# Seven raw weight buffers in place of four, in an encoder layer on one Trainium2 core

## The chip, the core and the metric

The kernel runs on one core of a Trainium2 chip. The core has a matrix engine (TensorE; PE in the profile, PEld for its weight loads), a vector engine (VectorE, DVE), a scalar engine (ScalarE, ACT), GpSimd (POOL), a queue engine that issues most transfers (SyncE, SP), and 16 DMA engines. The metric is the device time of one execution in microseconds (us), the median of several runs.

## What is computed

One layer of a hybrid streaming encoder, in float32, on 2048 prompt tokens and 128 sample tokens (8 sequences of 16), model width 1024:

```python
qm, km, vm, om, ip, fp, qa, ka, va = split_in(x @ w_in)
hm = sigmoid(om) * head_norm(mlstm_chunkwise(qm, km, vm, ip, fp))   # 4 heads of 128, matrix memory
ha = window_attention(rope(qa), rope(ka), va, attn_sinks)           # 8 q heads, 2 kv heads of 64, window 128
mix = concatenate([hm, ha]) @ w_out
h = layer_norm(ALPHA * x + mix)
u = h @ w_up                                                        # 1024 -> 2 * 2816
a, g = split(causal_conv(u, w_conv, b_conv))                        # width 3, per channel
y = layer_norm(ALPHA * h + (silu(g) * a) @ w_down)                  # 2816 -> 1024
```

The prompt starts from empty states, the sample from given ones (mLSTM state, key and value cache, last convolution rows). Outputs are y and the new states of both.

## The kernel before

**Tiles and stages.** The 2176 tokens are 17 tiles of 128. Four stages follow one another. (i) The *input projection* (some 0 to 620 us of the profile): four blocks of four tiles, the sample's with the first; per block five groups of columns and seven products per group (`i_product`, L704). The mLSTM, the attention and the sample's own work are woven between the products. (o) The *output projection* and the first layer norm (to about 900 us). (f) The *up-projection* with convolution and gate (about 900 to 1840 us): three blocks of tiles, 22 pairs of value and gate columns in each, seven products per pair (L1873). (d) The *down-projection* and second norm (to the end): three blocks, seven products, six units of the inner dimension in each (L2083).

**Precision and products.** A float32 product is made of three matmuls on reduced-precision parts (`mm3`): each operand is split into a high part (ScalarE casts, L217) and a low part (VectorE subtracts, L218). The large projections use schemes with seven block products in place of eight, so some of their operands are sums of quarters of a weight matrix or of the tokens. Sums that later blocks need again are kept in HBM (`zws`, `zw`, `zt`); `d_sums` (L844 to L856) makes those of w_down during stage (i), from loads of w_down into tiles `txy`.

**The way of a weight.** SyncE loads 4 KB per partition of raw weights into a tile of the tag `wraw`. L217 and L218 split it into two tiles of the tags `wlo` and `whi` (named w or uw; four buffers each, two more in an extra pool), and PE reads those. The raw tile is free again when the split has ended, the split tiles when PE has used them. Four places take a `wraw` tile:
- `warm_up` (L320), once, at the start;
- `raw_slot` (L405), which stages (i) and (o) use for w_in, the gate columns, w_out, kept sums and one sum of tokens (L547);
- `f_raw` (L1769), two tiles for each pair of stage (f): value weights `wv` (loaded at L1770) and gate weights `wg` (L1772, L1774), of which L1790 to L1793 form sums in the first block;
- `d_weights` (L2016), one for each unit of stage (d), loaded at L2019 five units ahead.

In stage (i) some raw tiles are also changed in place (L505, L508, L510, L522), where sums are formed.

**What sets the order.** The order of PE's instructions is written out by hand: a class `Chains` interleaves the chains of mLSTM, attention and sample with the products by costs and due times. For stages (i) and (o) the program asks for raw tiles ahead of their use: `next_raw` walks a list of weight units, and `raw_free` allows a request only when the older of the last four raw tiles are marked as done. The orders of VectorE, ScalarE, GpSimd and SyncE aren't written out: a list scheduler lays them down at build time, with its own estimates of durations, from the dependences and from when buffers come free. Each engine and each queue then runs its instructions in that order; an instruction that waits holds up all behind it.

**Beside the weights.** SyncE's queue also carries stores and reloads of everything that passes through HBM: projected queries, keys and gates, tokens, the first norm's inputs (L1635) and its gains (L1646), convolution rows (`cc`, `zc`), gated results (`zf`, reloaded as `r`). GpSimd issues three kinds of transfers itself: `zM` (L1078), which writes a row of the mLSTM's sums to HBM, `wi` (L1080), which broadcasts it back to all partitions and is read by VectorE's L1109, each 16 times, and finished tiles of y (L2126), 12 times.

**The instructions named by the prediction.** L771, L775, L777 (evictions of a product's bank in stage (i)), L761 (gates), L871 (rotary); L1132, L1150 to L1159 (the mLSTM's scores and head norm); L1307 to L1320 (softmax of the prompt's attention); L1501 to L1511 and L1517 (softmax and transposes of the sample's); L1902 to L1910 (convolution of stage (f)); L1894 (its gate).

[...]

Of the kernel before, what the change touches and what calls it, by code (L numbers as in the profile page):

```python
# [8 lines left out]
F32 = mybir.dt.float32  # L9
# [5 lines left out]
P = 128  # L15
D = 1024
KD = D // P
# [17 lines left out]
HOLDS = {"pm": 6500, "pgr": 4000, "pnum": 5000, "ppo": 6500}  # L35

WB = 4


IBLOCKS = [[0, 1, 2, 3, 16], [4, 5, 6, 7], [8, 9, 10, 11], [12, 13, 14, 15]]  # L40
# [164 lines left out]
class Prog:  # L205
# [111 lines left out]
    def warm_up(self):  # L317

        z = self.wp.tile([P, 512], F32R, name="zero", tag="wlo", bufs=WB)
        raw = self.wp.tile([P, 512], F32, name="zraw", tag="wraw", bufs=4)  # L320
        self.nc.vector.memset(raw, 0.0)
        self.nc.vector.tensor_copy(z, raw)
        self.raws[0][1] = True
        self.halves[0] += 1
        self.release(1)
        for i in range(9):
            self.nc.tensor.matmul(self.ib[i % 3], z[:, :P], z, start=i < 3, stop=i >= 6, skip_group_check=True)
# [9 lines left out]
    def i_begin(self):  # L337
# [45 lines left out]
        self.spare = False  # L383
        self.extra, self.ring, self.turn = None, 2 * WB, 0
        self.raws.append([None, False])
# [4 lines left out]
    def half(self, shape):  # L390
        n = self.halves[0]
        self.halves[0] += 1
        if self.extra is not None:
            e = (n - self.extra) % (2 * WB + 2)
            if e < 2:
                return self.wx.tile(shape, F32R, name="w", tag="wex", bufs=2)
        self.turn = 1 - self.turn
        return self.wp.tile(shape, F32R, name="w", tag=("wlo", "whi")[self.turn], bufs=WB)

    def unit_more(self, wx):  # L400
        self.wx, self.extra = wx, self.halves[0]
        self.ring = 2 * WB + 2

    def raw_slot(self, shape):
        e = [self.wp.tile(shape, F32, name="wraw", tag="wraw", bufs=4), False]  # L405
        self.raws.append(e)
        return e

# [1351 lines left out]
    def f_slot(self, dt=F32R):  # L1760
        self.slot = (self.slot + 1) % 10
        if self.slot < 8:
            return self.wp.tile([P, KD, P], dt, name="uw", tag=("whi", "wlo")[self.slot % 2], bufs=WB)
        return self.wx.tile([P, KD, P], dt, name="uw", tag="wex", bufs=2)

    def f_raw(self, b, j):

        nc = self.nc
        v, g = [self.wp.tile([P, KD, P], F32, name=n, tag="wraw", bufs=4) for n in ("wv", "wg")]  # L1769
        nc.sync.dma_start(v, self.a["wup"][j])  # L1770
        if b == 0:
            nc.sync.dma_start(g, self.a["wup"][NFF + j])  # L1772
        else:
            nc.sync.dma_start(g[:, 4:], self.a["wup"][NFF + j][:, 4:])  # L1774
        self.wr[b, j] = v, g
# [229 lines left out]
    def d_weights(self):  # L2005

        if self.nw >= len(self.dseq):
            return
        b, s, u = self.dseq[self.nw]
        self.nw += 1  # L2010
        ks = DUNITS[u]
        m, k0, c0 = {1: (None, 0, 0), 2: (None, NK2, 0), 3: (None, NK2, 512), 5: (0, 0, 0), 7: (0, 0, 512), 4: (1, 0, 0), 6: (1, 0, 512)}[s]
        src = self.a["wdn"] if m is None else self.zt[m]
        src = src[k0 + ks[0]:k0 + ks[-1] + 1, :, c0:c0 + 512].rearrange("k p n -> p k n")
        n = len(ks) * 512
        raw = self.wp.tile([P, 1024], F32, name="wraw", tag="wraw", bufs=4)  # L2016
        hi, lo = [self.f_slot().rearrange("p a b -> p (a b)") for _ in range(2)]
        v = lambda t: t[:, :n].rearrange("p (a b) -> p a b", b=512)
        self.nc.sync.dma_start(v(raw), src)  # L2019
        self.split(hi[:, :n], lo[:, :n], raw[:, :n])  # L2020
        self.dw[b, s, u] = v(hi), v(lo)
# [164 lines left out]
```

## Time and profile before

| | |
|---|---|
| device time, median of 3 runs | 2314.28 us (2314.28, 2314.28, 2319.7) |
| the profiled execution's own time | 2316.15 us |
| span of the profiled execution | 2314.3 us |
| mean granted clock of PE | 0.996 |
| PE busy, stage by stage (us of us) | 0–60: 52.3; 60–100: 40.0; 100–300: 198.4; 300–400: 95.4; 400–600: 197.8; 600–900: 298.2; 1000–1800: 798.0; 1800–1900: 97.4; 1900–2200: 300.0; 2200–2314: 105.5 |
| moved by DMA | 632.38 MB, mean 273 GB/s |
| busy share of the DMA engines | 0.97 at 300–400 and 500–600, 0.67 at 1900–2200 |

The profile shows one execution. "Busy" of PE includes the time in which a matmul is in flight. A row of the waits says which engine's instruction waited for which, in all, how often, and the longest; a row of the timeline gives start, duration, engine, line, operation, output<-inputs, shape, and in brackets the idle time ahead of it with what ended it. `<-DMA` means that a transfer's landing ended it. "SPq" is SyncE's queue of transfers. A row of the windows gives the stretch, its length, the busy time of PE, PEld, DVE, ACT and POOL (with instructions), PE's granted clock (1.00 is full speed), the DMA engines' busy share, and GB/s.

### The profile page before, as it was taken

How to read it: one execution, taken by the hardware profiler on the slowest of the kernel's cores; microseconds unless marked ns; L12 is line 12 of the kernel's file. 1: busy time of each engine (PE TensorE's matmuls, PEld its weight loads, DVE VectorE, ACT ScalarE, POOL GpSimd, SP SyncE). 2: the span in 40 equal slices, each digit the busy share in tenths (PEclk: the TensorE clock that was granted, in tenths of full speed). 3: DMA queues.
4: the chain of work that ended last, by engine and by line, in shares of the span. 5: the costliest groups of instructions: out<-in, count | busy, mean ns of one | idle time of the engine just before them, and what ended most of it. 6: DMA issues, size and time to landing. Idle time of an engine off the chain costs nothing.

```text
span 2314.3 us, 39788 instructions
## 1 busy us (share of the span) xinstructions
PE 2281.9 (99%) x14293; PEld 2094.9 (91%) x14293; DVE 1808.1 (78%) x3075; ACT 1269.0 (55%) x2377; POOL 279.5 (12%) x509
## 2 busy tenths in 40 slices
PE   8999999999999999999999999999999999999998
PEld 8999989989877778999999999999999978888876
DVE  8777687787688888998788777678766786895987
ACT  5453466776766655555656555555555544444442
POOL 0001000000011212121002000013111200100200
PEclk9999999999999999999999999999999999999999
DMA  7888999999977757888778889978898776756743
GB/s 276 287 308 297 301 309 336 314 310 342 315 269 240 240 201 270 303 319 311 276 289 274 306 304 311 315 264 287 312 294 261 225 282 208 261 175 215 255 157 108
DMA packets 300166, 632.38 MB, mean 273 GB/s; under 512 B 47869, under 2 KB 141121, under 8 KB 299969
## 3 DMA queue, kind: packets, MB, share of 16 engines
q1 hardware_dynamic: 295296, 616.14, 77.9%
q0 software_dynamic: 3520, 10.56, 1.4%
q10 hardware_dynamic: 1152, 3.15, 0.4%
q8 instruction: 113, 1.85, 0.3%
q14 instruction: 85, 0.69, 0.1%
HBM read 458.11 MB, written 171.64 MB: 272 GB/s over the span
## 4 chain that ended last, share of the span: by engine, by line
PE 76%; DVE 5%; DMA 4%; issue 2%; ACT 1%; SPq 0%; POOL 0%; DVEq 0%; ACTq 0%; POOLq 0%
PE dps L1873 19%; PE fup L1873 19%; PE dps L704 7%; PE dps L2083 6%; PE fht L2083 6%; PE fup L2083 6%; PE dps L222 2%; PE dps L224 2%; PE dps L223 2%; PE ppo L1348 1%; PE psc L1303 1%; PE ppt L1342 1%; DVE w L218 1%; PE fht L1697 1%; DMA txy<-wdn 0%
## 5 line engine op out<-in xcount | busy, mean ns | idle before, releaser
L1873 PE MATMUL dps<-hh,uw 128*128 128x384 f32 (+1 forms) x1848 | 478.7, 328 | 2.0 <-DVE u L1904 2.0
L1873 PE MATMUL fup<-hh,uw 128*128 128x384 f32 (+1 forms) x1848 | 478.2, 328 | 1.5 <-ACT ua L1894 1.5
L1873 PEld LDWEIGHTS dps<-hh,uw 128*128 128x128 f32 x1848 | 330.5, 188 | 2.2 <-DVE u L1904 2.2
L1873 PEld LDWEIGHTS fup<-hh,uw 128*128 128x128 f32 x1848 | 330.0, 188 | 2.0 <-ACT ua L1894 1.9
L1930 DVE SCALAR_TENSOR_TENSOR cc<-u,cw,cc 128x768 f32<-128x768 f32 (+1 forms) x264 | 258.1, 978 | 64.9 <-ACT cc L1928 55.5
L1873 PE MATMUL fup<-hl,uw 128*128 128x384 f32 (+1 forms) x924 | 302.5, 327 | 1.7 <-DVE hl L218 1.7
L1873 PE MATMUL dps<-hl,uw 128*128 128x384 f32 (+1 forms) x924 | 302.8, 328 | 0.0
L704 PE MATMUL dps<-w,oh 128*128 128x256 f32 x1344 | 254.3, 284 | 0.7 <-DVE zev L777 0.7
L217 ACT CAST uw<-wraw 128x1024 fp32r<-128x1024 f32 x126 | 123.0, 979 | 223.8 <-PE dps L2083 120.1
L218 DVE TENSOR_TENSOR w<-wraw,w 128x1024 fp32r<-128x1024 f32 (+2 forms) x167 | 189.4, 1141 | 56.1 <-ACT w L217 48.9
L217 ACT CAST w<-wraw 128x1024 fp32r<-128x1024 f32 (+2 forms) x167 | 163.0, 985 | 107.3 <-PE dps L704 38.9
L704 PEld LDWEIGHTS dps<-w,oh 128*128 128x128 f32 x1344 | 210.5, 188 | 11.8 <-issue 8.1
L218 DVE TENSOR_TENSOR uw<-wraw,uw 128x1024 fp32r<-128x1024 f32 x126 | 142.4, 1131 | 65.7 <-ACT uw L217 65.5
L704 PE MATMUL dps<-w,ol 128*128 128x256 f32 x672 | 187.8, 279 | 0.0
L704 PE MATMUL dps<-oh,w 128*128 128x256 f32 x896 | 170.9, 285 | 6.6 <-ACT mr L1153 3.8
L1873 PEld LDWEIGHTS fup<-hl,uw 128*128 128x128 f32 x924 | 173.5, 188 | 2.4 <-DVE hl L218 2.3
L2083 PE MATMUL fup<-uw,fu 128*128 128x512 f32 x726 | 174.2, 396 | 0.6 <-DVE uw L218 0.6
L1873 PEld LDWEIGHTS dps<-hl,uw 128*128 128x128 f32 x924 | 173.8, 188 | 0.0
L2083 PEld LDWEIGHTS fup<-uw,fu 128*128 128x128 f32 x726 | 136.6, 188 | 34.1 <-DVE uw L218 1.1
L2083 PE MATMUL dps<-uw,fu 128*128 128x512 f32 x660 | 165.3, 396 | 1.1 <-DVE uw L218 1.1
L1928 ACT ACTIVATE cc<-u,cw 128x768 f32<-128x768 f32 (+1 forms) x132 | 132.2, 1002 | 57.8 <-DVE u L1910 28.5
L704 PEld LDWEIGHTS dps<-oh,w 128*128 128x128 f32 x896 | 142.2, 191 | 13.1 <-ACT mr L1153 4.1
(318 smaller groups left out, 4567.0 us busy)
## 6 DMA issues: line engine op xcount, KB each, us to landing
uw<-zw SPq DMA_DIRECT2D x176, 512.0 KB, 5.1
zw<-uw SPq DMA_DIRECT2D x88, 512.0 KB, 3.7
w<-zws SPq DMA_DIRECT2D x72, 512.0 KB, 6.2
wv<-wup SPq DMA_DIRECT2D x66, 512.0 KB, 5.0
wraw<-wi SPq DMA_DIRECT2D x65, 512.0 KB, 5.1
wraw<-zt SPq DMA_DIRECT2D x60, 512.0 KB, 4.3
wraw<-wdn SPq DMA_DIRECT2D x45, 512.0 KB, 4.3
wraw<-wo SPq DMA_DIRECT2D x40, 512.0 KB, 4.5
```

The costliest lines, as they stand in the source:

```text
L217: nc.scalar.copy(hi, src)
L218: nc.vector.tensor_sub(lo, src, hi.bitcast(F32))
L222: mm(out, ah, bh, start=start, stop=False)
L223: mm(out, ah, bl, start=False, stop=False)
L224: mm(out, al, bh, start=False, stop=stop)
L704: mm(o, l, r, start=s in (1, 7) and c == k == i == 0, stop=k == 3 and i == 2, skip_group_check=True)
L1303: nc.tensor.matmul(ps[kvh][:, j, :nk], q[rs, j0 + j], k[rs, sel], start=i == 0, stop=i == 2)
L1342: nc.tensor.transpose(pp[:, j * P:(j + 1) * P], scs[j // 2][:, 2 * kvh + j % 2, kt * P:(kt + 1) * P], self.ident)
L1873: mm(ps, l[:, k], r[:, k], start=s in (1, 7) and k == 0 and i == 0, stop=k == 3 and i == 2, skip_group_check=True)
L1928: S.activation(c[:, v], u[:, 2:2 + n], AF.Identity, bias=w[3], scale=w[2])
L1930: V.scalar_tensor_tensor(c[:, v], u[:, i:i + n], w[i], c[:, v], op0=ALU.mult, op1=ALU.add)
L2083: mm(ps, l[:, k, c], r[:, k], start=s in (1, 4, 7) and u == 0 and k == 0 and i == 0, stop=u == nu - 1 and k == n - 1 and i == 2, skip_grou ...
```

## The change

The tag `wraw` gets seven buffers in place of four at its four places, through a new constant `WR`. The three more buffers are 4 KB per partition each. The program's scratch for GpSimd's transfers is set to 4 KB in place of 16. `raw_free` still counts by four, so the requests of stages (i) and (o) stand at the same places of the program as before, as do those of `f_raw` and `d_weights`.

```diff
@@ -35,6 +35,7 @@
 WB = 4
+WR = 7
@@ -317,7 +318,7 @@
-        raw = self.wp.tile([P, 512], F32, name="zraw", tag="wraw", bufs=4)
+        raw = self.wp.tile([P, 512], F32, name="zraw", tag="wraw", bufs=WR)
@@ -402,7 +403,7 @@
     def raw_slot(self, shape):
-        e = [self.wp.tile(shape, F32, name="wraw", tag="wraw", bufs=4), False]
+        e = [self.wp.tile(shape, F32, name="wraw", tag="wraw", bufs=WR), False]
@@ -1766,7 +1767,7 @@
     def f_raw(self, b, j):
-        v, g = [self.wp.tile([P, KD, P], F32, name=n, tag="wraw", bufs=4) for n in ("wv", "wg")]
+        v, g = [self.wp.tile([P, KD, P], F32, name=n, tag="wraw", bufs=WR) for n in ("wv", "wg")]
@@ -2013,7 +2014,7 @@
-        raw = self.wp.tile([P, 1024], F32, name="wraw", tag="wraw", bufs=4)
+        raw = self.wp.tile([P, 1024], F32, name="wraw", tag="wraw", bufs=WR)
@@ -2175,7 +2176,7 @@
-    nc = bacc.Bacc("TRN2", target_bir_lowering=False, num_devices=1)
+    nc = bacc.Bacc("TRN2", target_bir_lowering=False, num_devices=1, dynamic_dma_scratch_size=4096)
```

The changed order of each engine is known from the built program without running it. PE's is the same, row for row; those of VectorE, ScalarE, GpSimd and SyncE differ in many places.

## The prediction

> **What bounds the kernel now.** I read the page's first two parts, then the waits of the engines, then the stages, and last the instructions around each stall of TensorE (PE). Page:
>
> ```profile
> span 2314.3 us, 39788 instructions
> PE 2281.9 (99%) x14293; PEld 2094.9 (91%) x14293; DVE 1808.1 (78%) x3075; ACT 1269.0 (55%) x2377; POOL 279.5 (12%) x509
> ```
>
> PE is busy for 2281.9 of 2314.3 us. All that a better supply of data can return is the other 32.4 us, with the slow clock that follows some stalls. The change touches raw weight buffers, so the question is how many of those 32 us wait on them. SyncE's queue waits for them often, each row below being "a load of raw weights waited until VectorE's split (L218) freed a buffer":
>
> ```profile
> SPq L2019 <- DVE uw L218: 272.1, 101, 6.1
> SPq L455 <- DVE w L218: 71.7, 42, 6.3
> ```
>
> These are the two largest of that kind, 344 us together. PE's own waits look different (total, times, longest):
>
> ```profile
> PE dps L704 <- ACT mr L1153: 3.8, 1, 3.8
> PE dps L1873 <- DVE u L1904: 2.0, 1, 2.0
> PE fup L1873 <- DVE hl L218: 1.7, 2, 1.1
> PE dps L704 <- DVE w L218: 1.3, 2, 0.8
> PE dps L2083 <- DVE uw L218: 1.1, 1, 1.1
> PE dps L730 <- DVE w L218: 0.9, 2, 0.5
> PE dps L704 <- ACT w L217: 0.8, 1, 0.8
> PE fup L2083 <- DVE uw L218: 0.6, 1, 0.6
> ```
>
> No row has a load as releaser, and the five that name a weight split (w or uw) come to 4.7 us. So SyncE's 344 us are mostly slack: the loads wait, and PE doesn't wait for them. What PE loses lies in single stalls, and each has to be followed by itself.
>
> **The change part by part.** *PE's order* is identical in the two programs; only when its operands are ready can change. *Seven buffers* let the scheduler that lays down the other queues issue raw loads earlier and put the splits (ScalarE's L217, VectorE's L218) further ahead of other work. That moves instructions on SyncE, DVE and ACT; it adds none with a cost to PE.
>
> (a) *126 us.* Here the loads were late:
>
> ```profile
> 119.09 0.33 SPq L455 DMA_DIRECT2D wraw<-wi  x1
> 124.73 1.23 DVE L508 TENSOR_TENSOR wraw<-wraw 128x1024 f32<-128x1024 f32 x1 [2.63 <-DMA wraw<-wi]
> 126.61 0.39 PE L704 MATMUL dps<-w,oh 128*128 128x256 f32 x1 [0.73 <-DVE zev L777]
> ```
>
> The load issued at 119.09 lands near 124.7; DVE stands idle for 2.63 at L508, the eviction L777 behind it is late, and PE waits 0.73. With a buffer free earlier the load is there: **−0.7** (0 to −0.7).
>
> (b) *250 us.* The sample attention's softmax runs DVE L1503, L1506, L1510, then GpSimd L1511, then PE's L1517:
>
> ```profile
> 247.60 0.16 DVE L1503 SCALAR_TENSOR_TENSOR amx<-amx,k_sinkx 128x4 f32<-128x4 f32 x1
> 248.46 1.23 DVE L218 TENSOR_TENSOR w<-wraw,w 128x1024 fp32r<-128x1024 f32 x1 [0.30 <-DMA vn<-zkv]
> 251.87 0.33 PE L1517 MATMUL ppt<-ident,scs 128*128 128x128 f32 x1 [0.82 <-POOL scs L1511]
> ```
>
> In the changed order L871, the token sum L547 and the split L218 stand between L1503 and L1506. L871 stood just ahead of L1503 before; the other two are new there. L547 works on a tile of the size of the split's and is priced like it, so L1506 comes 2 × 1.23 = 2.5 later, and PE, which already waits 0.82, waits 3.3: **+2.5** (+0 if DVE reaches L1503 that much earlier, since much of its work has moved). A stall of that size can also halve PE's clock; below that is +1.5.
>
> (c) *330 us,* the largest stall:
>
> ```profile
> 317.74 0.38 SPq L844 DMA_DIRECT2D txy<-wdn  x1
> 324.48 0.98 ACT L1320 ACTIVATE sc<-sc,asm 128x128 f32<-128x128 f32 x3
> 325.20 0.69 DVE L850 TENSOR_TENSOR txy<-txy 128x512 f32<-128x512 f32 x1 [3.92 <-DMA txy<-wdn]
> 325.81 0.29 DVE L1150 BATCH_NORM_STATS2 bst<-pnum 128x6 f32<-128x128 f32 x1
> 328.63 0.17 ACT L1153 ACTIVATE mr<-pnum 128x2 f32<-128x2 f32 x1 [3.17 <-DVE bst L1150]
> 328.71 1.04 ACT L217 CAST w<-wraw 128x1024 fp32r<-128x1024 f32 x1
> 329.66 0.59 ACT L771 ACTIVATE zev<-dps 128x512 f32<-128x512 f32 x1
> 330.30 0.58 PE L704 MATMUL dps<-oh,w 128*128 128x256 f32 x1 [3.85 <-ACT mr L1153]
> ```
>
> DVE stands 3.92 at L850 for a w_down load; the head-norm statistics L1150 behind it are late, so ACT's L1153, so the eviction L771, and PE has no bank. In the changed order L850 stands behind the whole head-norm (after L1159): the first L1150 can run 3.9 + 0.7 earlier. What is late next is ACT itself, which stood idle from 325.46. In its changed order L771 comes behind L1153, three rows of L1320 (0.33 each) that used to come after it, and a split: 325.46 + 0.17 + 1.0 + 1.04 + 0.59 = 328.3 in place of 329.66 + 0.59 = 330.25: **−2.0** (−1, if the rows of L1320 wait for DVE's reciprocals ahead of them, to the whole −3.9).
>
> (d) *The clock.* The view by windows behind the ends of three stalls, and at full speed (the column after POOL is PE's granted clock):
>
> ```profile
> 330.30:333.30 3.00, 3.00 (x14) 3.00 (x15) 3.00 (x9) 1.86 (x6) 0.00 (x0) 0.51 1.16 348
> 1837.90:1841.20 3.30, 3.30 (x14) 3.20 (x15) 2.20 (x4) 0.92 (x2) 1.99 (x2) 0.59 0.40 146
> 1622.60:1625.90 3.30, 3.30 (x22) 3.30 (x23) 2.82 (x5) 1.76 (x4) 0.32 (x2) 1.00 0.49 147
> 333.30:336.30 3.00, 3.00 (x28) 3.00 (x28) 2.83 (x5) 2.44 (x8) 1.46 (x2) 1.00 1.00 354
> ```
>
> After 3.85 us of waiting 14 matmuls ran in 3 us where 28 run at full clock: 1.5 us lost. The 2.0 us of L1904 (1837.9) brought it too; after
>
> ```profile
> 1622.58 0.41 PE L1873 MATMUL fup<-hh,uw 128*128 128x320 f32 x1 [1.46 <-ACT ua L1894]
> ```
>
> it did not come. So between 1.5 and 2.0 us of waiting lies the price of another 1.5. The stall of (b), at 3.3, gets it: **+1.5**. That of (c) keeps about 1.9 and, I take it, its slow clock: 0 (−1.5 if not). [...]
>
> (e) *915 us,* the start of the up-projection:
>
> ```profile
> 892.77 0.33 SPq L1772 DMA_DIRECT2D wg<-wup  x1
> 897.05 0.69 DVE L1791 TENSOR_TENSOR uw<-wv,wg 128x512 f32<-128x512 f32 x1 [1.51 <-DMA wg<-wup]
> 915.24 0.45 PE L1873 MATMUL fup<-hl,uw 128*128 128x384 f32 x1 [1.11 <-DVE hl L218]
> ```
>
> The gate weights are asked for at 892.77, when a split has freed a buffer; DVE waits 1.51 for them and is then busy without a gap until the token split (hl, L218) for which PE waits 1.11 at 915.24. With seven buffers the load needs no free one and is there: **−1.1** (0 to −1.1).
>
> (f) *1882 us.* PE waits 0.6 (the last of PE's rows above) for a uw split that DVE runs behind a row of token sums:
>
> ```profile
> 1881.40 1.81 DVE L218 TENSOR_TENSOR uw<-wraw,uw 128x1024 fp32r<-128x1024 f32 x2
> ```
>
> In the new order that split stands ahead of several of them: **−0.6** (0 to −0.6). At 1837.9 DVE's order is unchanged, and so is the 2.0; the 1.1 near 2293 and the drain after it stay too, since what PE waits for there is arithmetic on DVE already behind.
>
> (g) *Everywhere else* ACT and DVE rows swap by one split (about 1.0 and 1.2 us each). PE's operands there are mostly several us early; where an eviction moves behind a split, it comes about 1 us later. I know of no excess of such places over the opposite ones: 0, with ±3.
>
> (h) *The smaller scratch.* GpSimd's transfers are few:
>
> ```profile
> L1078 POOL DMA_DIRECT2D zM<-r_M x16: 527/588/754, 284.3 to 802.7; - x16
> L1080 POOL DMA_DIRECT2D wi<-zM x16: 563/569/604, 287.6 to 807.8; - x16
> L2126 POOL DMA_DIRECT2D y<-yacc x12: 531/576/606, 1992.7 to 2191.5; - x12
> DMA to landing us min/median/max: 3.6/5.0/7.6
> ```
>
> I take **0**: 44 transfers in 2314 us, none of whose issues took over 0.76 us (ns, min, median, max), and whose broadcast (L1080, the last row) landed in 5.0: the row of log sums goes out to HBM and is awaited before it is broadcast back, and the results y follow one another, so one or two are in flight. The price if that is wrong is a rival below. The 3 × 4 KB of new buffers replace the 12 KB taken, so no other pool shrinks.
>
> *Sum:* −0.7 + 2.5 + 1.5 − 2.0 − 1.1 − 0.6 = **−0.4 us**; with the ends of each term −7.8 − 3 to +3.0 + 3. The profiled execution took 2316.15 us (1.85 around its span) and the median of the runs is 2314.28, so on the scale of the runs the forecast is 2314.28 − 0.4 ≈ **2314 us**, its own range 2303 to 2320.
>
> **Rivals.**
>
> *1. Slower: the head of SyncE's queue.* Loads issue in order, and with seven buffers more raw loads stand ahead of the loads for the first norm (L1635, L1646) and of the attention's. If a raw load still waits for a buffer there, DVE stands at a norm instruction, with the weight and token splits behind it. The place is 900 to 1000, where DVE has no room:
>
> ```profile
> 900.00:1000.00 100.00, 98.89 (x556) 97.08 (x555) 95.54 (x143) 56.94 (x95) 28.37 (x27) 1.00 0.79 286
> ```
>
> DVE is idle for 4.5 us there. A blocked load costs up to its wait for a buffer (6.3 at most, in SyncE's rows) and it decides from the point where the waits exceed those 4.5: three of them, 18.9 − 4.5 = 14.4, and one slow clock, 1.5: about 2330. For it: the orders of SyncE and DVE differ most there. Against it: the norm's instructions have moved back on DVE too, which gives their loads the same time.
>
> *2. Faster: the supply waits go.* If earlier splits ease ACT and DVE everywhere, the eight rows of PE's waits above go but for L1904's: 12.2 − 2.0 = 10.2, with the slow clock at 330, 1.5, and (b) doesn't come: 2314.28 − 11.7 ≈ 2303. Against it: most of those waits end on arithmetic, not on a load.
>
> *3. The buffers do nothing* but change order: SyncE's waits pass from buffers to the split tiles that PE frees, and (b) to (f) cancel or don't happen: 2314. It can't be told from the forecast by the time alone, and shares its chance.
>
> *4. The scratch binds.* If GpSimd held back each of its 16 broadcasts by one more landing of 5.0 us, and DVE, idle for 22% of the time by the page, passed on 78% of it: 16 × 5 × 0.78 = 62 us, 2376. [...]
>
> **How the numbers follow.** The forecast with rival 3: 0.60; rival 1, and smaller versions of it in the input stage: 0.22; rival 2: 0.15; rival 4: 0.03. A measurement of this kernel can tell about 0.3%, 7 us, from no change. Of the forecast's 0.60, 0.02 falls below and 0.02 above that; a third of rival 1 stays inside. Faster: 0.15 + 0.02 = 0.17; slower: 0.02 + 0.15 + 0.03 = 0.20; within: 0.63. The range leaves out rival 4 and half of what lies beyond 2326 and below 2303: **2303 to 2326**.
>
> **What would show it.** Right: SyncE's waits on L218 shrink by far more than PE's time; DVE's waits at L508 (124.7) and L1791 (897) gone; PE's stall near 252 grown to about 3 us with a clock of 0.5 behind it; that near 330 halved. Wrong: DVE idle at L1650 or L1635's consumers between 900 and 1000 with a load as releaser (rival 1); PE's waits on w, uw and mr gone (rival 2); GpSimd's issues L1078 and L1080 longer than their 0.6 us, or landing late (rival 4).

## The result, and the profile after

The changed kernel took 2309.16 us (median of 14 runs, 2305.68 to 2314.54) against 2317.41 us of the kernel before in the same sessions (14 runs): a ratio of 0.9968, 95% interval 0.9959 to 0.9977. By this ratio that is 7.4 us less, between 5 and 10; the two medians alone differ by 8.3. Timed again later (after_2 below) the ratio was 0.9964, 0.9951 to 0.9976. The profiled execution of the changed kernel has a span of 2304.4 us against 2314.3. The forecast was 2314 us, 0.4 less than the 2314.28 that three runs of the kernel before had given.

Lines of the changed kernel are one higher than before from L38 on. Its page, some of its PE waits, and four rows of SyncE's waits:

```profile
span 2304.4 us, 39746 instructions
PE 2279.1 (99%) x14293; PEld 2093.5 (91%) x14293; DVE 1807.5 (78%) x3075; ACT 1272.6 (55%) x2377; POOL 272.7 (12%) x509
```

```profile
PE ppt L1518 <- POOL v L1094: 2.9, 1, 2.9
PE dps L1874 <- DVE u L1905: 2.1, 1, 2.1
...
PE dps L2084 <- DVE uw L219: 1.1, 1, 1.1
PE dps L705 <- ACT mr L1154: 0.9, 1, 0.9
PE fup L1874 <- DVE hl L219: 0.9, 2, 0.6
```

```profile
SPq L2020 <- DVE uw L219: 269.1, 99, 6.1
...
SPq L1771 <- DVE uw L219: 47.8, 47, 2.6
SPq L456 <- DVE w L219: 44.1, 32, 4.8
...
SPq L462 <- DVE w L219: 29.6, 19, 3.5
```

PE's waits have changed in single places: 3.8 us on L1153 have become 0.9 on L1154, the wait for the sample's softmax has grown to 2.9, and those for L1894 and for uw in the fup banks are gone. SyncE's waits for raw buffers have changed by stage. In the down-projection they are as long as before: 272.1 us before, 269.1 now. In stages (i) and (o) they fell by a third: L455 and L461 had 71.7 and 35.6 us before, the same two loads (L456 and L462) have 44.1 and 29.6 now. I read the first as a queue that runs ahead until its buffers are full and then waits for a free one, at either depth; no run tests that.

**Where the time went.** PE's order is the same in all these kernels, so the start of the same matmul can be compared between two traces. This table gives, for stretches of the first profile of before, how much longer (+) or shorter (-) PE took from the matmul at one edge to that at the other. before_2 and scratch4 are two more profiles with the orders of the kernel before, after_2 a second one of the changed kernel, seven_io an experiment below.

| stretch, us | before_2 | scratch4 | after | after_2 | seven_io |
|---|---|---|---|---|---|
| 2–60 | -0.96 | +1.40 | +1.37 | -0.96 | -0.58 |
| 100–200 | -1.11 | -0.07 | -1.11 | -1.11 | -1.11 |
| 200–300 | +0.11 | +0.25 | +1.71 | +3.08 | +1.71 |
| 300–400 | -1.39 | -0.26 | -3.87 | -3.92 | -4.04 |
| 400–600 | -0.59 | +1.80 | -1.41 | -0.23 | -0.57 |
| 600–700 | +1.14 | +1.85 | -1.90 | -1.87 | -1.87 |
| 700–1000 | +0.21 | +0.17 | -0.73 | -0.71 | -0.56 |
| 1000–1600 | +0.01 | +0.19 | +0.34 | +0.37 | +0.07 |
| 1600–1700 | -0.99 | -0.75 | -1.89 | -1.89 | -1.79 |
| 1700–1860 | -1.53 | -0.01 | -1.36 | +0.16 | -1.54 |
| 1860–1900 | +0.01 | +0.01 | -0.85 | -0.85 | +0.01 |
| 1900–end | +0.03 | 0.00 | -0.16 | -0.19 | +0.05 |

Two executions with the same orders differ by up to 2.4 us in a stretch, and by 10 us in all. So the change is best read as the mean of its two profiles less the mean of the three of before: -0.7 at 100–200, +2.3 at 200–300, -3.3 at 300–400, -1.2 at 400–600, **-2.9 at 600–700**, -0.8 at 700–1000, +0.3 at 1000–1600, -1.3 at 1600–1700, -0.9 at 1860–1900, the rest within 0.2; -8.8 together, beside 7 to 8 by the timed runs.

### The profile page after: what moved, and what is told of

The parts are those of the page before. It is cut to its first block, busy times and chain, and to the rows that moved or that the text cites. A ratio compares the mean times of both kernels' runs of the same rounds, so it can differ in the third digit from the quotient of the medians.

```text
span 2304.4 us, 39746 instructions
## 1 busy us (share of the span) xinstructions
PE 2279.1 (99%) x14293; PEld 2093.5 (91%) x14293; DVE 1807.5 (78%) x3075; ACT 1272.6 (55%) x2377; POOL 272.7 (12%) x509
## 3 DMA queue, kind: packets, MB, share of 16 engines
q8 instruction: 113, 1.85, 0.3%
## 4 chain that ended last, share of the span: by engine, by line
PE 81%; DVE 4%; DMA 1%; issue 1%; ACT 1%; POOL 0%; SPq 0%; DVEq 0%; ACTq 0%; POOLq 0%
PE dps L1874 19%; PE fup L1874 19%; PE dps L705 7%; PE fup L2084 7%; PE dps L2084 6%; PE fht L2084 6%; PE dps L223 3%; PE dps L224 2%; PE dps L225 2%; PE ppo L1349 1%; PE psc L1304 1%; PE ppt L1343 1%; PE dps L731 1%; PE fht L1698 1%; DVE w L219 1%
## 5 line engine op out<-in xcount | busy, mean ns | idle before, releaser
L218 ACT CAST uw<-wraw 128x1024 fp32r<-128x1024 f32 x126 | 123.2, 978 | 231.4 <-PE dps L2084 122.4
L218 ACT CAST w<-wraw 128x1024 fp32r<-128x1024 f32 (+2 forms) x167 | 163.0, 984 | 121.3 <-PE dps L705 63.4
L2084 PEld LDWEIGHTS dps<-uw,fu 128*128 128x128 f32 x660 | 123.8, 188 | 31.5 <-DVE uw L219 1.5
```

What stands on the lines that cost most here:

```text
L218: nc.scalar.copy(hi, src)
L2084: mm(ps, l[:, k, c], r[:, k], start=s in (1, 4, 7) and u == 0 and k == 0 and i == 0, stop=u == nu - 1 and k == n - 1 and i == 2, skip_grou ...
```

## The experiments

My theory was that single stalls go, partly because loads come earlier and partly because rows change places. The rivals were that the depth of supply itself gives the time (SyncE's long waits), that part comes from the scratch, and, as the runs went on, that PE's gain at one place is taken back at the next.

**scratch4**, the scratch alone:

```diff
-    nc = bacc.Bacc("TRN2", target_bir_lowering=False, num_devices=1)
+    nc = bacc.Bacc("TRN2", target_bir_lowering=False, num_devices=1, dynamic_dma_scratch_size=4096)
```

> Four raw buffers as before, only the scratch of GpSimd's transfers cut from 16 to 4 KB; every engine's order is that of the kernel before. Theory (single stalls go because raw loads come earlier and rows move): no change, within 0.15% of before, and the issues of L1078 and L1080 as short as before (medians 588 and 569 ns). Rival (the scratch has a price that the buffers pay back): slower by some us, longer issues or later landings of GpSimd's transfers.

Ratio 1.000, interval 0.9989 to 1.0011. The issues of its GpSimd transfers, in the views of the two lines (ns, min, median, max):

```profile
L1078 POOL DMA_DIRECT2D zM<-r_M x16: 528/588/754, 285.6 to 807.6; - x16
L1080 POOL DMA_DIRECT2D wi<-zM x16: 566/570/604, 288.4 to 813.0; - x16
```

They are as short as before (588 and 569). The scratch shows no price here.

**seven_io** and **seven_fd**: seven buffers in one half of the kernel. Three tiles of the tag are allocated and kept by tiny GpSimd instructions, from the first raw weights of the up-projection to the end, or from the start up to there:

```diff
+ self.held = [self.wp.tile([P, 1024], F32, name="held", tag="wraw", bufs=WR) for _ in range(3)]
+ ... one GpSimd instruction per tile where the stretch begins, and one that reads it where it ends
```

> Seven raw buffers in stages (i) and (o); from the first raw weights of the up-projection on, three of them are held by tiles that nothing uses, so that four are left. Theory: PE's stalls of the first 900 us stand as with seven buffers (126, 330 and 657 us eased, 250 us larger), those after 900 us as before the change (915, 1622 and 1882 us): about 6.6 us less than before in the profile, -0.28%. Rival (the gain is SyncE's long waits for raw buffers, most of them in the down-projection): no gain here.

> Three of the seven raw buffers are held by tiles that nothing uses until the first raw weights of the up-projection have landed: four in stages (i) and (o), seven in (f) and (d). Theory: the stalls of the first 900 us as before the change, those at 915, 1622 and 1882 us gone: 0.8 + 1.7 + 0.9 = 3.4 us less than before in the profile, -0.15%. Rival (SyncE's waits for raw buffers, 272 us of them in the down-projection): the whole gain of 7 us, -0.3%, shows here.

seven_io: 0.9969 (0.9954 to 0.9985). seven_fd: 0.9989 (0.9980 to 0.9999). By these two ratios the gain is mostly from stages (i) and (o), where SyncE's waits for raw buffers are 107 us in all, and not from the down-projection, where they are 272. The supply rival, which put the gain there, is wrong. seven_fd loses the stall at 1882 us (-0.85, as expected), but 880 to 1000 us became 2.2 longer, I take it because the first pair of the up-projection is still loaded with three buffers held; so its 0.9989 is less than stages (f) and (d) give.

**sums4**: four buffers, and one order.

```diff
 (in d_sums)
+            with self.tc.issue_after(self.last_add) if k == 1 else nullcontext():
                 V.tensor_sub(x[:, l], x[:, r], x[:, l])   # and the three after it
 (in m_norm)
-        V.tensor_add(r, r, mv[:, :, 1])
+        self.last_add = V.tensor_add(r, r, mv[:, :, 1]).ins
```

> Four raw buffers and the scratch of before. Only one thing is moved: the second sum of w_down (VectorE L850 to L853, k = 1) is issued behind the head norm's L1159 of the first tile, as the changed order has it. Theory (the stall at 330 us is an order, not a supply): it shrinks from 3.85 to below 1.5 us and its slow clock goes, 3 to 4 us less than before in the profile, all of it between 320 and 340 us. Rival (the buffers cured it): the stall stays above 3 us.

The stall did go; PE's rows:

```profile
328.31 0.38 PE L704 MATMUL dps<-oh,w 128*128 128x256 f32 x1 [0.54 <-ACT zev L771]
...
335.95 0.33 PE L1177 MATMUL pht<-ident,hn 128*128 128x128 f32 x1 [0.44 <-ACT hn L1167]
336.77 0.33 PE L1177 MATMUL pht<-ident,hn 128*128 128x128 f32 x1 [0.49 <-ACT hn L1167]
...
369.28 0.39 PE L704 MATMUL dps<-w,oh 128*128 128x256 f32 x1 [0.76 <-ACT dps L799]
```

It fell from 3.85 to 0.54, and the clock behind it was 1.00 (328.0 to 331.3; 0.51 behind the stall of before). But the ratio is 0.9997 (0.9987 to 1.0008). In the trace PE is 4.7 us ahead of before by 335: 3.3 from the stall and 1.4 from the slow clock behind it. By 342 it has lost 3.6 of them, and by 370 the last 1.0. It waits at 335 to 337 for the head norm's scaling, and behind these short waits its clock is slow in this execution (0.56 and 0.59):

```profile
338.00:340.00 2.00, 2.00 (x11) 1.71 (x11) 1.78 (x2) 2.00 (x7) 0.00 (x0) 0.56 0.93 323
340.00:342.00 2.00, 2.00 (x9) 1.02 (x8) 1.45 (x5) 2.00 (x7) 0.00 (x0) 0.59 0.91 307
```

At the same matmuls the clock is 1.00 in before, before_2 and after, and after loses only 1.0 us there. So the order made the stall, as I had said. Curing it by itself showed no gain in the timed runs (at most 2.5 us by the interval); that PE lost all of it again within 40 us is seen in one execution, and in part by a slow clock that others didn't have.

**soft** and **soft_sums**: the changed kernel with priority for the sample's softmax, and the same with the edge of sums4.

```diff
+            with self.tc.high_priority():
                 V.scalar_tensor_tensor(mx, mx, 0.125, sk, op0=ALU.mult, op1=ALU.max)   # to L1511
```

> Seven buffers, with two orders set: the sample's softmax has priority, so that nothing but its own rows stands between L1503 and L1506, and the second sum of w_down stays behind the head norm (L850 after L1159), as the change put it. Theory (the change costs 2.0 us at 250 us by order alone): PE's wait at the sample's transposes goes from 2.9 to 0.8 us or less, 2 us less than with seven buffers alone in the profile, about -0.4% against before. Rival (that wait covers for late weights, and they come up next): the time of seven buffers alone, -0.3%.

> Seven buffers with priority for the sample's softmax alone. The order that follows from it puts the second sum of w_down (L850, k = 1) ahead of the head norm's L1150 again, as with four buffers, with the rest of the order nearly that of seven. Theory (the order of L850 is what made and cured the stall at 330 us): that stall is back with 3 to 4 us, between 320 and 350 us the time of before, less the 2 us of the softmax at 250: about +1.5 us against seven buffers alone, -0.25% against before. Rival (seven buffers bring the load of L850 earlier, and the stall goes by supply): no stall at 330, -0.4% against before.

soft_sums: 0.9972 (0.9960 to 0.9984); soft: 0.9967 (0.9953 to 0.9981). In both the 200–300 us stretch falls from +1.71 to -0.16, as expected of the order, and in both profiles later stretches are longer: 350 to 400 us is 0.8 and 1.3 longer than in after, 500 to 600 us 2.6 and 3.8. The sizes are not firm: late_fu (below), which has the orders of soft_sums up to 1822 us, is 2.0 and 1.5 longer there, after_2 is itself 1.2 longer than after at 500 to 600, and behind stalls near 514 us the clock of soft_sums and soft was slow (0.69 and 0.59). The time doesn't show the +2.3 of the change at 250 us either, but its intervals are about 3 us wide to each side. soft also tells how the stall at 330 us works. The rows of L851 (L850 before) in soft and in six (below), where it stands ahead of the head norm in both:

```profile
319.81 0.69 DVE L851 TENSOR_TENSOR txy<-txy 128x512 f32<-128x512 f32 x1 [1.96 <-DMA txy<-wdn]
```

```profile
324.07 0.69 DVE L851 TENSOR_TENSOR txy<-txy 128x512 f32<-128x512 f32 x1 [4.43 <-DMA txy<-wdn]
```

In soft VectorE waits 1.96 us for the load and PE 0.83 behind it, in six 4.43 and 3.14. So either cures the stall, an early load or a later L850. My expectation that soft would have it back was wrong.

**ask7** and **six**: requests seven tiles ahead, and six buffers.

```diff
-        n = 3 if self.spare else 4
-        return len(self.raws) < n or all(e[1] for e in self.raws[-4:len(self.raws) - n + 1])
+        n = 6 if self.spare else 7
+        return len(self.raws) < n or all(e[1] for e in self.raws[-7:len(self.raws) - n + 1])
```

```diff
-WR = 7
+WR = 6
```

> Seven buffers, and the requests of stages (i) and (o) allowed up to seven tiles ahead in place of four. Theory (with seven buffers the loads of stage (i) are no longer what PE waits for): within 0.1% of seven buffers alone, -0.3% against before, or a little slower where SyncE's queue is full of early loads (300 to 400 and 500 to 600 us, DMA engines 0.97 busy). Rival (supply still binds in stage (i)): faster than seven buffers alone by over 2 us.

> Six raw buffers in place of seven, all else as in the change. Theory (single stalls and orders): the order differs again in many places, so the terms at 126 and 915 us stay (the load is early with any buffer more), and those of order at 250 and 330 us may fall either way: between -0.1 and -0.4%. Rival (depth of supply): between four and seven, near -0.2%.

ask7: 0.9971 (0.9961 to 0.9981); six: 0.9971 (0.9960 to 0.9981). Both have the stall at 330 us (3.2 and 3.1 us) and are, within their intervals, as fast as the change. Neither more depth nor more asking shows a gain, and the seventh buffer none over the sixth.

**before_2, after_2 and sum8**: both kernels again, and the stall at 657 us.

> The kernel before, profiled again, to tell what belongs to its program from what changes with the execution. By the three kernels that have its order up to 900 us: the stalls at 126, 252, 330, 657, 915 and 1882 us come again (GpSimd's L1160 near 652 us takes 3.6 us again), as they are fixed by the order. Those that move with the execution: the slow clock in the first 20 us, behind 1838 us, and the stall at 1622 us.

> The kernel with seven buffers, profiled and timed again. If the gain belongs to the program: -0.3% again; no stall at 126, 657, 915 and 1882 us; GpSimd's L1160 near 648 us at 1.9 us. If part of it was the luck of one execution: some of these stalls are back, or the clock is slow behind the stall at 1830 us.

> Four buffers; the first instruction (L850) of the ninth sum of w_down (k = 8) is taken out of the row of VectorE's instructions near 653 us and put behind a later eviction. Theory for the stall at 657 us: GpSimd's L1160 (4 numbers per partition, about 1.0 us alone) gets on only when VectorE leaves its row of SBUF-to-SBUF instructions, so it takes 3.63 - 0.6 = 3.0 us here and PE's wait at 657 us falls from 1.65 to about 1.05. Rival (L1160 takes what it takes, or its input is late): 3.6 us and the same wait.

before_2 kept the stalls at 252, 330, 657, 915 and 1882 us, but not that at 126: 100–200 us was 1.11 shorter, as in the changed kernel. That one belongs to some executions with four buffers, and to none that was profiled with more. The stall at 1622 us was 0.35 in place of 1.46, and gone in scratch4, so it moves with the execution, as expected. after_2 gave 0.9964 (0.9951 to 0.9976); 126, 657 and 1882 stayed gone, and 915 was 0.33 in both profiles of the change.

The largest term, 657 us, was in no step of the prediction. GpSimd raises the head norm's four variances per partition to a power (L1160); ScalarE and PE wait behind it. GpSimd, VectorE and PE in the kernel before:

```profile
652.26 3.63 POOL L1160 TENSOR_TENSOR ms<-mr,mhalf 128x4 f32<-128x4 f32 x1 [6.92 <-DVE mr L1159]
```

```profile
652.02 1.22 DVE L218 TENSOR_TENSOR w<-wraw,w 128x1024 fp32r<-128x1024 f32 x1
653.16 0.69 DVE L850 TENSOR_TENSOR txy<-txy 128x512 f32<-128x512 f32 x1
653.76 1.22 DVE L218 TENSOR_TENSOR w<-wraw,w 128x1024 fp32r<-128x1024 f32 x1
654.90 0.68 DVE L1612 SCALAR_TENSOR_TENSOR ymix<-ymix,dps 128x512 f32<-128x512 f32 x1
```

```profile
657.72 0.55 PE L1342 MATMUL ppt<-ident,sc 128*128 128x128 f32 x3 [1.65 <-ACT pth L1343]
```

and in the changed one:

```profile
647.76 1.89 POOL L1161 TENSOR_TENSOR ms<-mr,mhalf 128x4 f32<-128x4 f32 x1 [5.74 <-DVE mr L1160]
```

```profile
647.52 1.22 DVE L219 TENSOR_TENSOR w<-wraw,w 128x1024 fp32r<-128x1024 f32 x1
649.67 0.69 DVE L851 TENSOR_TENSOR txy<-txy 128x512 f32<-128x512 f32 x1 [0.93 <-DMA txy<-wdn]
```

and in sum8, where L850 is out of the row (GpSimd, VectorE, PE):

```profile
649.71 3.03 POOL L1160 TENSOR_TENSOR ms<-mr,mhalf 128x4 f32<-128x4 f32 x1 [6.43 <-DVE mr L1159]
```

```profile
649.48 2.35 DVE L218 TENSOR_TENSOR w<-wraw,w 128x1024 fp32r<-128x1024 f32 x2
651.75 0.68 DVE L1615 SCALAR_TENSOR_TENSOR ymix<-ymix,dps 128x512 f32<-128x512 f32 x1
```

```profile
654.58 0.66 PE L1342 MATMUL ppt<-ident,sc 128*128 128x128 f32 x4 [0.56 <-ACT pth L1343]
```

In all three GpSimd ends 0.91 us after VectorE's row of instructions with both operands in SBUF: 654.98 and 655.89, 648.74 and 649.65, 651.83 and 652.74. Taking 0.6 us out of the row took 0.6 off L1160 (3.03 in place of 3.63), as expected. PE's wait fell by 1.1, more than expected; but with the same 3.63 it was 1.65, 2.79, 1.96 and 1.39 in before, before_2, scratch4 and sums4, and sum8 ran only once, so the size of that fall is not settled. The 0.91 are the same with the eviction behind the row (L1612, one operand in a bank, 654.90 to 655.58) and in the changed kernel, where VectorE waits from 648.74 on. In the changed kernel VectorE's order at this place is the same as before, but it waits 0.93 for a load of w_down in the middle of the row, and GpSimd is through in 1.89. So, by the traces, the largest gain comes from a load that is *late*. seven_fd, with the order of four buffers there, has it too: VectorE waited 1.24 us for that load, and L1160 took 1.89. The same instruction took 3.63 us beside the unbroken row and 1.89 where VectorE waited in it; why the row holds GpSimd up, no run shows.

**late_fu**: soft_sums, and two splits moved at the end of the up-projection.

```diff
-            if left in (8, 7, 5, 3, 1):
-                self.d_weights()
-            if left in (9, 8, 7, 6):
-                self.d_tokens()
+            with self.tc.issue_after(self.last_u) if left == 2 else nullcontext():   # L1904's instruction
+                if left in (8, 7, 5, 2, 1):
+                    self.d_weights()
+                if left in (9, 8, 7, 2):
+                    self.d_tokens()
```

> soft_sums, and at the end of the up-projection a split of raw weights and one of tokens, which stood ahead of the last sums of the gate (VectorE L1903 and L1905 of the kernel before it), are put behind them. Theory (late in the kernel nothing takes back what PE gains): PE's wait there falls from 2.1 to about 0.6 us, 1.5 us less than soft_sums between 1800 and 1860 us in the profile, and the rest to the end as in soft_sums; -0.3 to -0.4% against before. Rival (the splits are then late for the down-projection): the 1.5 us come back between 1840 and 1900 us.

```profile
1833.57 0.42 PE L1877 MATMUL dps<-hh,uw 128*128 128x320 f32 x1 [0.58 <-DVE u L1908]
1859.78 0.50 PE L2087 MATMUL fup<-uw,fu 128*128 128x512 f32 x1 [0.62 <-ACT fht L2095]
```

The wait fell to 0.58, and 1800 to 1860 us became 1.4 shorter than in soft_sums; a later wait of 0.62 gave 0.9 of it back (1860 to 1900 us), most of it, as the rival said. The ratio is 0.9950 (0.9931 to 0.9969), the lowest of all; its interval overlaps those of the changed kernel, so that it beats the kernel before is shown, and that it beats the change is not.

## Why the prediction was right or wrong

The measured time lies in the range, and its sign is the forecast's; the size is not: 0.4 us were forecast and 7 to 8 came, at the edge of what I had called the same. The range also holds the time of the kernel before, so lying in it says little. By the mean of the profiles steps (a) to (f) come to -2.8 in place of -0.4, and the rest, put at 0, to -6.0. Step by step:

- **(a) 126 us**, -0.7: mean -0.7 in the table. The mechanism is right; that the number fits is luck, for the stretch is 1.1 shorter where the stall goes, and the stall belongs to some executions only. The load is asked for at 110.65 in place of 119.09, and L509 (L508 before) no longer waits; SyncE's row and VectorE's:

```profile
110.65 0.33 SPq L456 DMA_DIRECT2D wraw<-wi  x1
```

```profile
118.16 1.22 DVE L509 TENSOR_TENSOR wraw<-wraw 128x1024 f32<-128x1024 f32 x1
```

- **(b) 250 us**, +2.5 and +1.5 for the clock: +2.3 in the mean. Right in its mechanism; the wait grew by 2.0 (2.85 in place of 0.82), and the slow clock came in one of two executions (0.52 in after_2, 1.00 in after). The row below names L1094 because that short instruction of GpSimd ended last; it runs right behind the softmax's L1512 (L1511 before). In the time the term couldn't be told (soft_sums).

```profile
254.15 0.33 PE L1518 MATMUL ppt<-ident,scs 128*128 128x128 f32 x1 [2.85 <-POOL v L1094]
```

- **(c) 330 us**, -2.0: -2.6 for 320 to 350 us in the mean. L850 went behind the head norm as forecast; ScalarE's rows, and PE's:

```profile
325.20 0.15 ACT L1154 ACTIVATE mr<-pnum 128x2 f32<-128x2 f32 x1
327.95 0.59 ACT L772 ACTIVATE zev<-dps 128x512 f32<-128x512 f32 x1
```

```profile
328.60 0.38 PE L705 MATMUL dps<-oh,w 128*128 128x256 f32 x1 [0.95 <-ACT mr L1154]
```

  0.95 us were left, not 1.9, and no slow clock followed (1.00 from 328.6 to 331.9). I had taken the gain as kept; sums4, which cures this stall alone, and six and ask7, which keep it and are as fast, show no time for it.

- **(d) the clock.** I read a threshold between 1.5 and 2.0 us out of three stalls. In the profiles of this case the length alone, between 1.63 and 3.21 us, doesn't tell whether the clock is slow behind a stall. The stall of 2.0 to 2.1 us near 1835 us left a clock of 0.59 in before; behind it, and behind that at 250 us, the windows of before_2, after_2 and after, in this order, show:

```profile
1834.30:1837.60 3.30, 3.30 (x19) 3.04 (x20) 3.21 (x6) 1.59 (x3) 2.01 (x2) 1.00 0.38 134
```

```profile
251.80:255.00 3.20, 3.19 (x16) 2.89 (x17) 0.00 (x0) 1.05 (x2) 0.00 (x0) 0.52 0.71 273
1830.80:1834.10 3.30, 3.30 (x14) 3.21 (x15) 2.50 (x5) 0.83 (x2) 1.22 (x2) 0.66 0.57 212
```

```profile
254.10:257.40 3.30, 3.25 (x28) 3.18 (x29) 0.00 (x0) 1.87 (x3) 0.04 (x1) 1.00 0.84 306
1830.60:1833.90 3.30, 3.30 (x19) 3.02 (x20) 3.21 (x6) 1.47 (x2) 1.18 (x2) 1.00 0.54 203
```

  That is 1.00 in before_2, 0.52 and 0.66 in after_2, 1.00 and 1.00 in after. The same stall slows the clock in one execution and not in the next. Over all 14 profiles, from 100 us on, 34 stalls were between 1.63 and 3.21 us long; behind 12 of them the clock of the next 3.3 us was 0.5 to 0.7, and the shortest of these was 1.63; behind the other 22 it was full, and the longest of these was 3.21. What decides between the two, no run shows.

- **(e) 915 us**, -1.1: about -0.9. **(f) 1882 us**, -0.6: -0.9. Both right: with six or seven buffers there, (f)'s stall is gone in every profile and 0.33 us of (e)'s are left. With four, (f)'s is always 0.64, but (e)'s was 1.1 to 1.3 in most, 0.71 in sums4 and 0.37 in sum8.

- **(g) everywhere else, 0 with ±3:** the step that failed. 657 us (-2.9), 1622 us (-1.3) and 400 to 600 us (-1.2) are 5.4 of the 8.8 us. At 1622 us ScalarE's rows, before and after:

```profile
1621.28 0.93 ACT L1928 ACTIVATE cc<-u,cw 128x656 f32<-128x656 f32 x1 [4.40 <-DMA zf<-cc]
1622.12 0.40 ACT L1894 COPY ua<-fup 128x320 f32<-128x320 f32 x1
```

```profile
1612.04 0.43 ACT L1895 COPY ua<-fup 128x320 f32<-128x320 f32 x1 [0.75 <-PE fup L1874]
1614.34 0.94 ACT L1929 ACTIVATE cc<-u,cw 128x656 f32<-128x656 f32 x1 [1.87 <-DMA zf<-cc]
```

  L1928 waits for a store of zf to land, and the eviction L1894 stood behind it. The changed order has the eviction first. That could have been seen in the two orders, which I had compared closely only around the stalls that I expected to move. But the order alone didn't make the stall: before_2 and scratch4, with the order of before, waited 3.28 and 2.82 us for the store in place of 4.40, and PE 0.35 and not at all, and seven_io and six have the eviction behind as well and no stall there. The 657 us could not have been read from VectorE's order, which is the same there; when the load lands decided it.

- **(h) the scratch**, 0: right (1.000).

- **Rivals.** The head of SyncE's queue (1) did not come: between 900 and 1000 us PE is busier than before (99.67), with VectorE at 96.08. Rival 2's size was nearer than the forecast's, but not its reason: PE's waits on w splits were about as large as before, and what went were single stalls of other kinds.

```profile
900.00:1000.00 100.00, 99.67 (x567) 98.86 (x566) 96.08 (x147) 58.26 (x97) 24.08 (x29) 1.00 0.80 290
```

One test that I had named came out as written and says little: of SyncE's waits on L218, the two rows of the prediction shrank from 343.8 to 313.2 us, far more than PE's time, all but 3 us of that in stage (i), and rival 2 would have shown it as well.

What stays open: what the terms up to 600 us, -3.0 in the mean, are worth one by one. The profiles of sums4, soft and soft_sums show a stall cured there and later stretches longer; how much of that the order takes back, and how much is the clock and the execution, wasn't settled. Nor was the 657 us stall cured by itself in the kernel before and timed, so that it is the largest term is read from the traces.

## What to carry to other kernels

More buffers, where a scheduler lays down the order, are first of all another order on every engine: compare the two orders over the whole kernel, for rows that wait on a load or a store ahead of an eviction, not only at the stalls that the change aims at. What the order doesn't tell is when loads and stores land, and that made or cured the stalls at 657 and 1622 us. Don't book a stall at its length: the one at 330 us, cured alone, showed no gain in the time, and of the 1.4 us gained at 1838 us in late_fu 0.9 were gone 40 us later, while those at 915 and 1882 us stayed gone. Profile the same program two or three times before a difference of 2 us at one place is explained.

## What the runs showed of the hardware

- A GpSimd instruction on 128x4 numbers (L1160) took 3.63 us beside VectorE's unbroken row of SBUF-to-SBUF instructions (the same in before, before_2, scratch4 and sums4) and ended 0.90 to 0.91 us after it (before, scratch4, sums4); with the row 0.6 us shorter it took 3.03 (sum8), and with a wait of VectorE of 0.93 (after) or 1.24 us (seven_fd) in the middle of the row 1.89.
- Behind PE stalls of 1.6 to 3.2 us the granted clock of the next 3.3 us was 0.5 to 0.7 in 12 of 34 cases and full in 22, also in executions of one program (near 1835 us 0.59 in before, 1.00 in before_2). In sums4 it fell to 0.56 behind three waits of 0.34 to 0.49 us within 2 us.
- Profiled spans of programs with the same orders lay between 2309.2 and 2318.8 us (before, before_2, scratch4).
